# Attention probabilities copied by DMA and transposed as float32r in a hybrid encoder step

## The chip, the cores and the metric

The kernel runs on one core of a Trainium2 chip. A core has a matrix engine (TensorE; PE in the profile, its weight loads PEld), a vector engine (VectorE, DVE), an activation engine (ScalarE, ACT), a general engine (GpSimd, POOL) and a queue engine (SyncE, SP) that here issues nearly all transfers; 16 DMA engines move the data. The metric is the device time of one execution in microseconds (us), the median of several. TensorE works from the on-chip memory SBUF and writes to the accumulators, PSUM; the other engines read PSUM from there.

Two types matter. Both have four bytes. A tile of type float32 ("F32") is multiplied by TensorE at full precision. A tile of type float32r ("F32R") is multiplied with a shortened mantissa. The kernel keeps nearly float32 accuracy in its projections by splitting each operand into a high and a low F32R part and adding three products.

## The reference, cut to what matters

One layer: a pre-normed input of 1024 new rows and 32 rows of running streams is projected to queries, keys, values, forget gates, the conv input and four gates. Attention and a causal convolution module run side by side, are gated, projected, mixed and added to the input. What the change touches is causal attention with 16 heads of width 64:

```python
def fox_attend(q, k, v, cq, ck, qpos, kpos):
    s = jnp.einsum('bqhd,bkhd->bhqk', q.astype(jnp.float32), k.astype(jnp.float32))
    bias = jnp.transpose(cq, (0, 2, 1))[:, :, :, None] - jnp.transpose(ck, (0, 2, 1))[:, :, None, :]
    mask = qpos[:, None] >= kpos[None, :]
    s = jnp.where(mask[None, None], s + bias, jnp.finfo(jnp.float32).min)
    p = jax.nn.softmax(s, axis=-1)
    o = jnp.einsum('bhqk,bkhd->bqhd', p, v.astype(jnp.float32))
    return o.astype(v.dtype)
...
def layernorm(x, g, b):
    xf = x.astype(jnp.float32)
    mu = jnp.mean(xf, axis=-1, keepdims=True)
    xc = xf - mu
    y = xc * lax.rsqrt(jnp.mean(xc * xc, axis=-1, keepdims=True) + EPS) * g.astype(jnp.float32) + b.astype(jnp.float32)
    return y.astype(x.dtype)
```

## The kernel before, in words

The program has three stages. In the first (up to about 605 us) the input is normed and transposed, and the projections for the conv input, the values, the keys, the queries and the attention gates are made; their results go to scratch tensors in HBM (`s_q`, `s_k`, `s_v`, `s_ga`). In the second (about 605 to 1100 us) attention runs, and the projections of the other three gates are mixed into it as filling work for TensorE. In the third the three output projections run.

**The attention loop.** `seq` holds 128 `Block`s, eight per head: block `i` has the 128 queries from row 128·i and the (i+1)·128 keys up to the diagonal. Four `Sample`s for the running streams are put between them. TensorE's order in this stage is the order in which the code is written (`manual_schedule(engines={E.PE})`); the queues of ACT, DVE, POOL and SP are set by a scheduler that runs while the kernel is built. Step `n` of the loop does four things: it starts the scores of block n+3, turns the probabilities of block n, runs four steps of the filler (`fill(4)`: twelve matmuls of a gate projection, line L102, with the single PSUM buffer of the pool `pq`), and, two steps after every fourth block of a head, multiplies by the values.

**One block.** `Block.scores` (L905, L906) puts the scores into one of two PSUM buffers (tag `S`). DVE adds the diagonal mask (L908) and takes the row maximum (L910). ACT takes the exponential into an SBUF tile `P` of type F32 and sums the rows (L913); `P` has three buffers. DVE inverts the sums (L915) and POOL scales `P` in place (L916). `Block.turn` transposes `P` in pieces of 128 by 128 (L926): TensorE loads the piece as its weights and streams the 128 columns of the identity `ident` through it. ACT and DVE copy the result to `pt` (L929). `Block.values` multiplies `pt` by `V` (L940), both F32. All 16 heads together have 16·36 = 576 pieces.

**What is loaded.** `Head.load` brings one head's queries and keys in eight transfers of up to 256 KB (L768 to L775), five steps ahead, and for each second head the values of two heads, `V` (L778, two buffers). The result of two heads goes to `s_o` (L953). The gate results go out by L754, and the weights of the filler come in by L85. All these share SP's queue, which issues in order: a transfer that waits for its data or its buffer holds up those behind it.

**The convolution in the attention stage.** The taps of the last conv input (f = 7) run on DVE during attention, one at a time, as the filler's `beat()` allows. The tile `shift`, subtracted from the conv output before the sums of the layer norm, is read back from `s_m` into a tile of its own at the start of the stage.

Of the kernel before, what the change touches and what calls it, by code (L numbers as in the profile page):

```python
# [48 lines left out]
def build(tc, xT, xt, wv, wf, ckT, cv, clT, stT, vec, cst, yT, kT, vO, lfO, cpT, csT):  # L49
# [195 lines left out]
    def sums(f):  # L245
        return [lambda: from_shift(f, sides["y", f]), lambda: into_sums(f, sides["y", f])]
# [104 lines left out]
    nc.vector.memset(eps_t, EPS)  # L351
    ident = cp.tile([128, 128], F32, name="ident")
    smask = cp.tile([128, TS], F32, name="smask")
# [83 lines left out]

    nc.vector.tensor_copy(ident, cst_t[:, C_ID:C_ID + 128])
    u0 = u_tile(0)
# [318 lines left out]
    class Head:  # L758
# [3 lines left out]
        def load(self):  # L762
# [12 lines left out]
            nc.sync.dma_start(f32(KA[64:68]), s_ak[h])  # L775
            if h % 2 == 0:
                self.V = heads[h + 1].V = hp.tile([128, 8, 128], F32, name="V", tag="V")
                nc.sync.dma_start(self.V, s_v[:, :, 64 * h:64 * h + 128].rearrange("b t d -> t b d"))  # L778

# [27 lines left out]
    cvt[0] = pool("cv7", 1, stack=p2, side="right")  # L807
    taps.extend(last + sums(7))
    psS = pool("psS", 2, stack=p2, space=PS)
# [78 lines left out]
    class Block:  # L888
# [5 lines left out]
        def scores(self):  # L894
# [15 lines left out]
            nc.vector.tensor_reduce(nm[:, 0:1], ps[:, :nb, :w], axis=AX.XY, op=ALU.max, negate=True)  # L910
            self.P = P = ap.tile([128, T], F32, name="P", tag="P", bufs=3)
            with tc.issue_after(sides["tables"].ins):
                nc.scalar.activation(P[:, :nk].rearrange("p (b w) -> p b w", b=nb), ps[:, :nb, :w], AF.Exp,  # L913
                                     bias=nm[:, 0:1], accum_out=nm[:, 1:2])
            nc.vector.reciprocal(nm[:, 2:3], nm[:, 1:2])  # L915
            nc.gpsimd.tensor_scalar(P[:, :nk], P[:, :nk], nm[:, 2:3], 1.0, op0=ALU.mult, op1=ALU.mult)  # L916

        def turn(self):
            i, P = self.i, self.P
            pt_ = PT[i // 4]  # L920
            qo = slice((i % 4) * 128, (i % 4) * 128 + 128)
            for u in range((i + 4) // 4):
                nj = min(4, i + 1 - 4 * u)
                pt = psT.tile([128, 512], F32, name="ptr2", tag="T")
                for j in range(nj):
                    nc.tensor.transpose(pt[:, 128 * j:128 * j + 128],  # L926
                                        P[:, 128 * (4 * u + j):128 * (4 * u + j) + 128], ident)
                put = nc.vector.tensor_copy if u else nc.scalar.copy
                put(pt_[:, 4 * u:4 * u + nj, qo], pt[:, :128 * nj].rearrange("p (j q) -> p j q", j=nj))  # L929

        def values(self):
# [20 lines left out]
            if e == 1 and c == 1:  # L952
                nc.sync.dma_start(s_o[self.head.h // 2, :, :T], ot)  # L953

    PT = [ap.tile([128, 4 * n, 512], F32, name=f"pt{n}", bufs=1) for n in (1, 2)]
# [26 lines left out]
    def layernorm():  # L982

        shift = sides["shift"]
        for _ in range(4):
# [3 lines left out]
        def put(sl, ps):  # L989
            t = t352("t", 3)  # L990
            nc.scalar.activation(t, mean[:, sl], AF.Square)
            nc.vector.scalar_tensor_tensor(rstd[:, sl], ps, 1.0 / D, t, op0=ALU.mult, op1=ALU.subtract)
            nc.vector.tensor_add(mean[:, sl], mean[:, sl], shift[:, sl])
            nc.vector.tensor_scalar(rstd[:, sl], rstd[:, sl], EPS, None, op0=ALU.add)
# [15 lines left out]
    ln = layernorm()  # L1010
    sides["shift"] = ap.tile([128, TT], F32, name="shift", bufs=1)
    nc.sync.dma_start(sides["shift"], s_m)
    start(seq[0])
    fill(8)
    start(seq[1])
    fill(4)
    start(seq[2])
    for n, b in enumerate(seq):
        if n + 3 < len(seq):
            start(seq[n + 3])  # L1020
        if n + 5 < len(seq) and getattr(seq[n + 5], "i", 1) == 0:
            seq[n + 5].head.load()
        if n + 6 < len(seq) and isinstance(seq[n + 6], Sample):
            seq[n + 6].load()
        if isinstance(b, Sample):
# [221 lines left out]
```

## Time and profile before

| what | value |
|---|---|
| time, median of 3 runs | 1402.85 us (1401.42 to 1404.89) |
| the profiled execution | 1405.11 us, its span 1403.3 us |
| granted TensorE clock, mean | 0.999 |
| TensorE busy, whole span | 1390.1 us (99%) |
| TensorE busy from 612 to 1090 us | 476.77 of 478 us |
| DMA share from 612 to 1090 us | 0.46, 129 GB/s |
| transposes of `P` | 576, mean record 273 ns, busy 84.2 us together |

The span is the profiled time from the first to the last instruction; the profiled execution's own time is 1.8 us longer. A record of a matmul begins when its operands are fetched, and its end is modelled, so records of neighbours overlap. What one matmul costs in a stream is therefore read from the distance of starts, not from the length of a record.

### The profile page before, as it was taken

Reading aid. Unit: us, or ns where it says so; the run is one execution under the profiler, and the core shown is the slowest. Engines: PE = TensorE matmul, PEld = TensorE weight load, DVE = VectorE, ACT = ScalarE, POOL = GpSimd, SP = SyncE. Lnnn points to the kernel's source line nnn. Section 1 sums busy time; section 2 is a strip of 40 time slices with the busy share of each in tenths; the row PEclk is TensorE's granted clock in tenths of the full one; section 3 lists DMA queues with packets and bytes.
Section 4 is the critical chain, followed back from the end, with each engine's and each line's share of the span. In section 5 each row is a group of like instructions: output and inputs, shape, how many; then the busy total and the mean of one; then the engine's idle time right before and its main releaser. Section 6 shows DMA issues by size and latency. Waiting matters only on the chain.

```text
span 1403.3 us, 23422 instructions
## 1 busy us (share of the span) xinstructions
PE 1390.1 (99%) x8999; PEld 1303.6 (93%) x8999; DVE 866.0 (62%) x1199; ACT 604.2 (43%) x1180; POOL 617.5 (44%) x541
## 2 busy tenths in 40 slices
PE   8999999999999999999999999999999999999999
PEld 7999999999999999998888888878888999999998
DVE  6687787888898998646655656644444497132111
ACT  6322334646464642245454546544554455232100
POOL 2324254557585875343433433232332366254320
PEclk9999999999999999999999999999999999999999
DMA  4242333424342484335545546353532778444431
GB/s 181 92 141 92 119 108 99 160 76 142 106 152 92 138 194 150 111 100 129 148 107 160 146 136 177 101 154 109 155 115 73 276 254 271 143 138 142 150 108 47
DMA packets 102288, 192.77 MB, mean 137 GB/s; under 512 B 17248, under 2 KB 70368, under 8 KB 102176
## 3 DMA queue, kind: packets, MB, share of 16 engines
q1 hardware_dynamic: 102032, 191.21, 44.4%
q8 instruction: 71, 1.16, 0.4%
q14 instruction: 41, 0.34, 0.1%
q10 hardware_dynamic: 144, 0.07, 0.0%
HBM read 125.58 MB, written 65.64 MB: 136 GB/s over the span
## 4 chain that ended last, share of the span: by engine, by line
PE 92%; issue 3%; DVE 2%; ACT 2%; POOL 1%; DMA 1%; SPq 0%; ACTq 0%; POOLq 0%; DVEq 0%
PE pj L102 67%; PE pjv L582 7%; PE po L940 5%; PE ptr L926 4%; PE psS L905 3%; PE psS L906 2%; POOL wl L94 1%; PE pst L698 1%; PE pst L697 1%; PE po L885 0%; DVE y L1082 0%; PE ptx L427 0%; DMA xtok<-xt 0%; ACT xh L429 0%; PE pjs L541 0%
## 5 line engine op out<-in xcount | busy, mean ns | idle before, releaser
L102 PE MATMUL pj<-xh,wh 128*128 128x352 f32 (+2 forms) x1536 | 510.0, 332 | 1.7 <-ACT t L753 1.1
L102 PE MATMUL pj<-xh,wl 128*128 128x352 f32 (+2 forms) x1536 | 494.0, 322 | 1.9 <-POOL wl L94 1.9
L102 PE MATMUL pj<-xl,wh 128*128 128x352 f32 (+2 forms) x1536 | 495.5, 323 | 0.2
L94 POOL TENSOR_TENSOR wl<-raw,wh 128x384 fp32r<-128x384 f32 (+1 forms) x258 | 323.1, 1280 | 258.1 <-ACT wh L91 226.9
L258 DVE SCALAR_TENSOR_TENSOR y<-u,vec_t,y 128x1086 f32<-128x1086 f32 x240 | 382.5, 1594 | 23.7 <-ACT y L255 19.6
L102 PEld LDWEIGHTS pj<-xh,wh 128*128 128x128 f32 x1536 | 289.0, 188 | 10.2 <-ACT t L753 6.6
L102 PEld LDWEIGHTS pj<-xh,wl 128*128 128x128 f32 x1536 | 289.9, 189 | 2.5 <-POOL wl L94 2.2
L102 PEld LDWEIGHTS pj<-xl,wh 128*128 128x128 f32 x1536 | 289.1, 188 | 1.4 <-DVE xl L430 1.2
L916 POOL TENSOR_SCALAR P<-P,nm 128x128 f32<-128x128 f32 (+7 forms) x128 | 107.6, 842 | 283.3 <-DVE nm L915 216.9
L91 ACT CAST wh<-raw 128x1024 fp32r<-128x1024 f32 x86 | 90.1, 1048 | 111.2 <-PE pj L102 80.5
L913 ACT ACTIVATE P<-psS,nm 128x128 f32<-128x128 f32 (+7 forms) x128 | 95.4, 745 | 70.7 <-DVE nm L910 61.5
L910 DVE TENSOR_REDUCE nm<-psS 128x1 f32<-128x128 f32 (+7 forms) x128 | 96.8, 756 | 8.6
L908 DVE TENSOR_TENSOR psS<-psS,cmask 128x128 f32<-128x128 f32 x128 | 38.1, 297 | 100.3 <-PE psS L906 99.3
L929 ACT COPY pt<-ptr 128x512 f32<-128x512 f32 (+3 forms) x128 | 65.0, 508 | 75.8 <-PE ptr L926 75.1
L715 POOL TENSOR_TENSOR ql<-qn,qh 128x352 fp32r<-128x352 f32 (+1 forms) x48 | 66.0, 1374 | 68.0 <-ACT qh L714 54.9
L926 PE MATMUL ptr<-ident,P 128*128 128x128 f32 x576 | 84.2, 273 | 0.0
L940 PE MATMUL po<-pt,V 128*64 128x512 f32 (+1 forms) x384 | 75.8, 530 | 0.0
L926 PEld LDWEIGHTS ptr<-ident,P 128*128 128x128 f32 x576 | 69.1, 140 | 5.6 <-issue 0.4
L582 PE MATMUL pjv<-vwh,xh 128*128 128x260 f32 x256 | 72.5, 283 | 0.0
L582 PE MATMUL pjv<-vwl,xh 128*128 128x260 f32 x256 | 72.4, 283 | 0.0
L582 PE MATMUL pjv<-vwh,xl 128*128 128x260 f32 x256 | 72.3, 282 | 0.0
L905 PE MATMUL psS<-KB,QB 128*128 128x256 f32 (+2 forms) x192 | 70.1, 366 | 0.6 <-ACT t L751 0.6
(200 smaller groups left out, 2237.4 us busy)
## 6 DMA issues: line engine op xcount, KB each, us to landing
raw<-wf SPq DMA_DIRECT2D x88, 512.0 KB
QB<-s_q SPq DMA_DIRECT2D x32, 256.0 KB
KB<-s_k SPq DMA_DIRECT2D x32, 256.0 KB
kT<-qn SPq DMA_DIRECT2D x8, 528.0 KB
s_ga<-t SPq DMA_DIRECT2D x24, 176.0 KB
s_gb<-t SPq DMA_DIRECT2D x24, 176.0 KB
s_ma<-t SPq DMA_DIRECT2D x24, 176.0 KB
s_mb<-t SPq DMA_DIRECT2D x24, 176.0 KB
```

Source lines behind the costliest of these rows:

```text
L91: nc.scalar.copy(wh, raw)
L94: nc.gpsimd.tensor_sub(wl[:, k0:k1, :], raw[:, k0:k1, :], f32(wh[:, k0:k1, :]))
L102: nc.tensor.matmul(ps, a[:, kt, :], b(kt, sl), start=(first and n == 0), stop=(last and n == N - 1))
L258: t = nc.vector.scalar_tensor_tensor(y, u[:, i:i + CW], w, y, op0=ALU.mult, op1=ALU.add)
L582: nc.tensor.matmul(ps[:, :VC], a, b, start=(n == 0), stop=(n == 23))
L715: nc.gpsimd.tensor_sub(ql[:, :n], qn[:, o], f32(qh[:, :n]))
L905: nc.tensor.matmul(ps[:, b, :wm], QB[:, qsl], KB[:, ksl], start=True, stop=False)
L910: nc.vector.tensor_reduce(nm[:, 0:1], ps[:, :nb, :w], axis=AX.XY, op=ALU.max, negate=True)
L913: nc.scalar.activation(P[:, :nk].rearrange("p (b w) -> p b w", b=nb), ps[:, :nb, :w], AF.Exp, bias=nm[:, 0:1], accum_out=nm[:, 1:2])
L916: nc.gpsimd.tensor_scalar(P[:, :nk], P[:, :nk], nm[:, 2:3], 1.0, op0=ALU.mult, op1=ALU.mult)
L926: nc.tensor.transpose(pt[:, 128 * j:128 * j + 128], P[:, 128 * (4 * u + j):128 * (4 * u + j) + 128], ident)
L940: nc.tensor.matmul(po[64 * o:64 * o + 64, q0:], V[:, j + o, hd], p[:, j + o, q0:], start=(j == 0), stop=(j == njb - 2), skip_group_check=True)
```

## The change

Five things are changed, all of them for the attention stage.

1. A new tile `R` of type F32R, three buffers. After POOL has scaled `P`, a transfer on SP's queue copies `P` to `R`, bit for bit (`f32(self.R[...])` is the same memory seen as F32). `P` has two buffers now.
2. `turn` reads `R`, and the transposes have F32R operands: `R` as weights, `ident_r` as the stream. The identity tile is now F32R, and `ident` is its F32 view for the other transposes.
3. Scores are started four blocks ahead. `Head.load` and `Sample.load` move by one step as well.
4. `V` has one buffer. Its load (`load_v`) is taken out of `Head.load`: the first stays there, the next ones are issued behind the values of the last block of two heads.
5. `shift` has no tile of its own. After the last tap of f = 7, `shift_again` reads it into the slot of that conv input, `u`.

```diff
-    ident = cp.tile([128, 128], F32, name="ident")
+    ident_r = cp.tile([128, 128], F32R, name="ident")
+    ident = f32(ident_r)
...
-            if h % 2 == 0:
-                self.V = heads[h + 1].V = hp.tile([128, 8, 128], F32, name="V", tag="V")
-                nc.sync.dma_start(self.V, s_v[:, :, 64 * h:64 * h + 128].rearrange("b t d -> t b d"))
+            if h == 0:
+                self.load_v()
+
+        def load_v(self):
+            h = self.h
+            self.V = heads[h + 1].V = hp.tile([128, 8, 128], F32, name="V", tag="V", bufs=1)
+            nc.sync.dma_start(self.V, s_v[:, :, 64 * h:64 * h + 128].rearrange("b t d -> t b d"))
...
-    taps.extend(last + sums(7))
+
+    def shift_again():
+        sides["shift"] = u7p.tile([128, UW], F32, name="u", tag="u")
+        nc.sync.dma_start(sides["shift"][:, :TT], s_m)
+        return 0.1
+
+    taps.extend(last + [shift_again] + sums(7))
...
-            self.P = P = ap.tile([128, T], F32, name="P", tag="P", bufs=3)
+            self.P = P = ap.tile([128, T], F32, name="P", tag="P", bufs=2)
...
             nc.gpsimd.tensor_scalar(P[:, :nk], P[:, :nk], nm[:, 2:3], 1.0, op0=ALU.mult, op1=ALU.mult)
+            self.R = ap.tile([128, T], F32R, name="R", tag="R", bufs=3)
+            nc.sync.dma_start(f32(self.R[:, :nk]), P[:, :nk])
 
         def turn(self):
-            i, P = self.i, self.P
+            i, P = self.i, self.R
...
-                    nc.tensor.transpose(pt[:, 128 * j:128 * j + 128],
-                                        P[:, 128 * (4 * u + j):128 * (4 * u + j) + 128], ident)
+                    nc.tensor.transpose(pt[:, 128 * j:128 * j + 128].bitcast(F32R),
+                                        P[:, 128 * (4 * u + j):128 * (4 * u + j) + 128], ident_r)
...
             if e == 1 and c == 1:
                 nc.sync.dma_start(s_o[self.head.h // 2, :, :T], ot)
+                if self.head.h < H - 1:
+                    heads[self.head.h + 1].load_v()
...
     start(seq[2])
+    start(seq[3])
     for n, b in enumerate(seq):
-        if n + 3 < len(seq):
-            start(seq[n + 3])
-        if n + 5 < len(seq) and getattr(seq[n + 5], "i", 1) == 0:
-            seq[n + 5].head.load()
-        if n + 6 < len(seq) and isinstance(seq[n + 6], Sample):
-            seq[n + 6].load()
+        if n + 4 < len(seq):
+            start(seq[n + 4])
+        if n + 6 < len(seq) and getattr(seq[n + 6], "i", 1) == 0:
+            seq[n + 6].head.load()
+        if n + 7 < len(seq) and isinstance(seq[n + 7], Sample):
+            seq[n + 7].load()
```

**TensorE at the start of the attention stage.** Before, the scores of blocks 2 and 3 (384 and 512 columns) and then the turn of block 0:

```order
L905 MATMUL psS<-KB,QB 128x384
L906 MATMUL psS<-KA,QA 128x384
L905 MATMUL psS<-KB,QB 128x512
L906 MATMUL psS<-KA,QA 128x512
L926 MATMUL ptr_6532<-ident,P 128x128
L102 MATMUL pj<-xh,wh 128x352
```

And with the change:

```order
L916 MATMUL psS<-KB,QB 128x384
L917 MATMUL psS<-KA,QA 128x384
L916 MATMUL psS<-KB,QB 128x512
L917 MATMUL psS<-KA,QA 128x512
L916 MATMUL psS<-KB,QB 128x320
L917 MATMUL psS<-KA,QA 128x320
L916 MATMUL psS<-KB,QB 128x320
L917 MATMUL psS<-KA,QA 128x320
L939 MATMUL ptr_6552<-ident,R 128x128
```

The scores of block 4 (two halves of 320 columns) now stand ahead of the first turn, and the turn reads `R`. The filler stands where it stood.

**SP's queue where a new pair of heads begins.** Before, around the load of `V` (`raw` is a filler weight, `s_ma` a gate result, `QB`, `KB`, `QA`, `KA` the next head; numbers tell buffers apart):

```order
L85 DMA raw_9614<-wf 128x1024
L754 DMA s_ma_64<-t_9094 128x352
L778 DMA V_9567<-s_v_59 128x8x128
L953 DMA s_o_70<-ot_8316 128x1024
L950 DMA ga_9683<-s_ga_66 128x1024
L768 DMA QB_9556<-s_q_57 64x1024
L754 DMA s_ma_64<-t_9249 128x352
L769 DMA QB_9556<-s_q_57 64x1024
L770 DMA KB_9558<-s_k_58 64x1024
```

And with the change:

```order
L783 DMA V_10020<-s_v_59 128x8x128
L929 DMA R_9986<-P_9982 128x768
L85 DMA raw_10559<-wf 128x1024
L966 DMA s_o_70<-ot_9106 128x1024
L846 DMA kc_10053<-ckT 128x2x512
L769 DMA QB_10414<-s_q_57 64x1024
L770 DMA QB_10414<-s_q_57 64x1024
L771 DMA KB_10416<-s_k_58 64x1024
L772 DMA KB_10416<-s_k_58 64x1024
L773 DMA QA_10413<-s_q_57 64x1024
L929 DMA R_10039<-P_10035 128x896
```

The copies of `P` stand among the loads: that of the block with 896 keys has five pieces of a head's queries and keys, a cache load and `s_o` right ahead of it.

**ACT's queue in the same stage**, with what each instruction waits for (a name that begins with DMAHW is a transfer). Before:

```order
L945 COPY ot_9009<-po_9676 64x512 [waits PE_49]
L929 COPY pt2_6437<-ptr2_9699 128x4x128 [waits PE_49]
L913 ACTIVATE P_9695,nm_9693<-psS_9689,nm_9693 128x256 [waits DVE_49,PE_49,Pool_49]
L929 COPY pt2_6437<-ptr2_9738 128x4x128 [waits PE_49]
L913 ACTIVATE P_9734,nm_9732<-psS_9728,nm_9732 128x384 [waits DVE_49,PE_49,Pool_49]
L753 COPY t_9762<-pj_9710 128x352 [waits PE_49]
```

And with the change:

```order
L942 COPY pt2_6437<-ptr2_9870 128x4x128 [waits PE_49]
L924 ACTIVATE P_9864,nm_9862<-psS_9858,nm_9862 128x384 [waits DMAHW1_49,DVE_49,Pool_49]
L942 COPY pt2_6437<-ptr2_9909 128x4x128 [waits PE_49]
L924 ACTIVATE P_9903,nm_9901<-psS_9897,nm_9901 128x512 [waits DMAHW3_49,DVE_49,Pool_49]
L754 COPY t_9933<-pj_9881 128x352 [waits PE_49]
```

Each exponential now waits for a transfer, the copy that frees its buffer of `P`, and the filler's copies out of PSUM (L753, now L754) stand behind exponentials in the same queue.

More of the change, by code (lines that the diff above doesn't have):

```diff
@@ L436, in x_split @@
                 behind.pop(0)()
-    nc.vector.tensor_copy(ident, cst_t[:, C_ID:C_ID + 128])
+    nc.vector.tensor_copy(ident_r, cst_t[:, C_ID:C_ID + 128])
     u0 = u_tile(0)
@@ L982, in layernorm @@
     def layernorm():
-        shift = sides["shift"]
         for _ in range(4):
@@ L992, in put @@
             nc.vector.scalar_tensor_tensor(rstd[:, sl], ps, 1.0 / D, t, op0=ALU.mult, op1=ALU.subtract)
-            nc.vector.tensor_add(mean[:, sl], mean[:, sl], shift[:, sl])
+            nc.vector.tensor_add(mean[:, sl], mean[:, sl], sides["shift"][:, sl])
             nc.vector.tensor_scalar(rstd[:, sl], rstd[:, sl], EPS, None, op0=ALU.add)
@@ L1010, in build @@
     ln = layernorm()
-    sides["shift"] = ap.tile([128, TT], F32, name="shift", bufs=1)
-    nc.sync.dma_start(sides["shift"], s_m)
     start(seq[0])
```

## The prediction

> **What bounds the kernel now.** I read the page's head first, then the table of stages, then who waits in the attention stage, then TensorE's timeline.
>
> ```profile
> span 1403.3 us, 23422 instructions
> PE 1390.1 (99%) x8999; PEld 1303.6 (93%) x8999; DVE 866.0 (62%) x1199; ACT 604.2 (43%) x1180; POOL 617.5 (44%) x541
> 612.00:1090.00 478.00, 476.77 (x3119) 405.07 (x3119) 263.31 (x582) 240.95 (x531) 169.30 (x192) 1.00 0.46 129
> 960.00:1000.00 40.00, 39.96 (x254) 34.24 (x253) 18.68 (x46) 20.71 (x46) 13.57 (x18) 1.00 0.68 182
> PE pj L102 <- ACT t L753: 0.8, 1, 0.8
> ```
>
> The third and fourth lines are stretches (start:end, length, busy time of PE, PEld, DVE, ACT and POOL, granted clock, DMA share, GB/s); the last is the only wait of PE between 612 and 1090 us. TensorE hardly waits there, at full clock, and DVE, ACT and POOL are busy for at most 55% of the stage. So the stage lasts as long as TensorE's instructions need, and a nanosecond taken off each of the 576 transposes is 0.576 us off the end, until something else comes late.
>
> **What a transpose costs, and why.** Distances of starts count, not lengths of records.
>
> ```profile
> L926 PE MATMUL ptr<-ident,P 128*128 128x128 f32 x576 | 84.2, 273 | 0.0
> 904.94 1.04 PE L926 MATMUL ptr<-ident,P 128*128 128x128 f32 x8
> 280.89 0.60 PE L636 MATMUL ptr<-ident,lf 128*16 128x128 f32 x4
> 280.74 0.47 PEld L636 LDWEIGHTS ptr<-ident,lf 128*16 128x16 f32 x4
> L926 PEld LDWEIGHTS ptr<-ident,P 128*128 128x128 f32 x576 | 69.1, 140 | 5.6 <-issue 0.4
> 14.70 0.28 PE L102 MATMUL pj<-xh,wh 128*128 128x256 f32 x1
> 14.82 0.28 PE L102 MATMUL pj<-xh,wl 128*128 128x256 f32 x1
> 14.94 0.28 PE L102 MATMUL pj<-xl,wh 128*128 128x256 f32 x1
> 42.75 0.35 PE L102 MATMUL pj<-xl,wh 128*128 128x416 f32 x1
> ...
> 43.31 0.35 PE L102 MATMUL pj<-xl,wh 128*128 128x416 f32 x1
> L102 PE MATMUL pj<-xh,wl 128*128 128x352 f32 x1488 | 478.4, 322 | 1.9 <-POOL wl L94 1.9
> L978 PE MATMUL psn<-mean,ones_f 128*128 128x352 f32 x6 | 2.4, 476 | 0.0
> ```
>
> Eight transposes last 1.04 us from the first start to the last end; less one record of 0.273 that is seven steps, so (1.04 − 0.273)/7 = 0.110 us each. Four transposes of the forget gates (L636) give the same (0.60 − 0.27)/3 = 0.11 us, though their weights have 16 columns and not 128. So the weight load does not set the step; the 128 streamed columns do, at 0.11/128 = 0.86 ns a column.
>
> The F32R matmuls of L102 stream cheaper: 0.12 us for 256 columns, and (43.31 − 42.75)/3 = 0.187 us for 416. The line through both has (0.187 − 0.12)/160 = 0.42 ns a column, half of the above. L978 agrees: a plain F32 matmul of 352 columns leaves two records (six for three matmuls) of 476 ns where F32R leaves one of 322, and the extra 154 ns are again 0.44 ns a column. F32 streams each column twice, F32R once.
>
> **The change part by part.**
>
> *Transposes as F32R.* The line goes on to 0.12 − 128·0.42 ns = 0.066 us at 128 columns. No row has F32R with fewer than 256 columns, so this is bounded from both sides: at best the transpose halves wholly, 0.055 us; at worst short streams lose the F32R rate and cost what a plain F32 matmul does, two records of two passes, 2·0.110 = 0.22 us. I take 0.066, the end of the line that four widths make. 576·(0.110 − 0.066) = 25.3 us off; the bounds give 31.7 us off and 63 us on.
>
> The Trainium skill ("TensorE: Matmul & The Clock Gate", section "Back-to-back issue gap") gives about 81 ns per matmul for a stream of pairs of weight load and 128-column matmul. By that the transposes would save 576·(0.110 − 0.081) = 16.7 us, an estimate from the page; its figure is not for F32R, and the rows above neither show nor exclude it.
>
> *The copies.* 128 copies of 64 to 512 KB, 4 bytes·128 rows·128 columns·576 = 37.7 MB. In the stage 129 GB/s take a DMA share of 0.46, so 37.7 MB over 478 us (79 GB/s) add about 0.28: 0.74 on average and 0.96 in the fullest stretch above. TensorE does not wait for bytes but for the last copy of its block. What covers a copy is the time between POOL's end and the turn:
>
> ```profile
> 922.67 0.39 PE L905 MATMUL psS<-KB,QB 128*128 128x512 f32 x1
> 927.04 1.53 POOL L916 TENSOR_SCALAR P<-P,nm 128x1024 f32<-128x1024 f32 x2 [2.47 <-DVE nm L915]
> 934.47 1.04 PE L926 MATMUL ptr<-ident,P 128*128 128x128 f32 x8
> 935.59 0.48 ACT L913 ACTIVATE P<-psS,nm 128x256 f32<-128x256 f32 x1
> 987.12 1.91 POOL L916 TENSOR_SCALAR P<-P,nm 128x768 f32<-128x768 f32 x2
> 989.59 0.60 PE L926 MATMUL ptr<-ident,P 128*128 128x128 f32 x4
> 0.74 0.86 SPq L325 DMA_DIRECT2D xtok<-xt  x2
> 4.80 1.06 ACT L380 ACTIVATE sq<-xtok 128x1024 f32<-128x1024 f32 x1 [2.35 <-DMA xtok<-xt]
> ACT sma L1125 <- DMA sma<-s_ma: 16.4, 9, 4.7
> 923.56 0.45 SPq L768 DMA_DIRECT2D QB<-s_q  x1
> SPq L754 <- ACT t L753: 174.3, 44, 9.3
> ```
>
> In the usual case (first three lines) POOL is done by 928.6 and the turn starts at 934.47: at least 5.9 us of slack. In the worst that I found, POOL works two blocks off until 989.03 and the turn starts at 989.59: 0.6 to 1.5 us. Scores one block earlier add a mean step of (1090 − 612)/132 = 3.6 us to every slack: 9.5 usual, 4 to 5 worst. A copy costs, by the first load of the program, 4.80 − 0.74 = 4.1 us with another of the same size beside it. The nearest rows bound it: the 0.45 us of its issue alone at one end, and at the other 4.7 us, the longest that ACT waited for a 176 KB piece behind other loads. I take 3 us free and 5 to 8 us behind a head's eight loads, where 1.3 MB stand in the queue. That fits into 9.5 us and not always into 4 to 5. SP itself has room: 128·0.45 = 58 us of issuing against 174 us in which it waits for gate results; but a copy behind such a wait inherits it. I charge 3 us for a few late copies.
>
> *`P` with two buffers.* The exponential of block m+2 now waits for the copy of block m. In the rows above POOL leaves the block with 1024 keys by 928.6, and the exponential two blocks on (256 keys) starts at 935.59: 7 us for a copy of 3 us, hidden. If the copy takes 8 us, the exponential is late by a microsecond, and behind it on ACT stands the filler's copy out of the one buffer of `pq`, for which TensorE waits next. This is in the 3 us.
>
> *Scores four ahead.* Nothing is added to TensorE's work. At the start of the stage the scores of block 4 need the PSUM buffer of block 2:
>
> ```profile
> 612.58 0.40 PE L906 MATMUL psS<-KA,QA 68*128 68x512 f32 x1
> 613.47 0.58 ACT L913 ACTIVATE P<-psS,nm 128x384 f32<-128x384 f32 x1
> ```
>
> Block 3's scores are issued by 612.8, the exponential of block 2 ends at 614.05, and the turn of block 0 now stands behind: 1.2 us lost once. The first copy (POOL done at about 610) has until 615 and is hidden.
>
> *`V` with one buffer, `shift` in another's slot.* `V` is loaded behind the last values of its two heads, some four blocks (4·3.6 = 14 us) before its first use; a 512 KB load took 4.1 us above. `shift` holds DVE once for a load of that size; DVE is busy for 263 of 478 us. I cost both at nothing; without that cover they would be 4 us each, seven times and once.
>
> **The sum**, against the profiled execution's own 1405.1 us: 1405.1 − 25.3 + 3 + 1.2 = 1384.0. The median of the runs lies 2.3 us lower, so 1381.7: I say **1382 us**, 1.5% faster. With other sizes of the same case (0.055 to 0.075 us a transpose, 0 to 8 us of late copies) it lies between 1374 and 1392.
>
> **The rivals.**
>
> *Two passes whatever the type.* The transposes are a mode of their own: their 128-column weight loads take 140 ns, those of all other matmuls 188. If that mode and not the type sets two passes for four-byte data, the step stays 0.110 and the change only adds 3 + 1.2 us and some crowding: 1407 to 1411, say 1409, slower. It decides if the step measures above about 0.103 us, where 576 times the gain no longer pays the 4.2 us. Against it: the same two passes are seen outside the mode (L978), and F32R loses one there. Chance 0.15.
>
> *Late copies.* The copies wait in the loads' bursts, ACT's queue stops behind an exponential, and the filler's buffer is not emptied. Point from which it decides: copies that take over 9 us from POOL's end in most heads. For it: the DMA share of 0.96 in the fullest stretch and the order of SP's queue, which puts the two largest copies of a head behind 1.3 to 2.3 MB of loads. Against it: 40 us windows with 0.68 are the fullest, and usual slack is 9.5. Three blocks in each of 16 heads late by 0.3 us are 14 us: 1382 + 14 − 3 = 1393; by 1 us, 48 us, all that is won and more. Chance 0.15, of which 0.03 ends slower and 0.02 level. The Trainium skill ("DMA: Bandwidth & Descriptors", section "Queues, rings and completion order") says that each DMA engine takes the descriptors of a queue's ring in order; that is how a copy would inherit the loads ahead of it. No row here shows it by itself.
>
> *The weight load as a floor.* Each transpose has a load of its own. In this mode a load takes 140 ns for 128 columns and about 88 ns for 16 (L636: four in 0.47 us), so 128 columns are some 60 ns of it, close to the 54 ns that the F32R stream would need. If the two overlap only in part, the step ends between 0.066 and 0.110; the middle, 0.088, takes 576·0.022 = 12.7 us off: 1405.1 − 12.7 + 4.2 − 2.3 = 1394. Against it: at 256 columns loads of 188 ns run at a step of 0.12 without a sign of it. Chance 0.12.
>
> The page's 81 ns, above, would be such a floor; by it the time would be 1390, an estimate.
>
> *Short F32R streams at the full F32 cost.* 0.22 us a transpose: 576·0.110 = 63 us on: 1405.1 + 63 + 4.2 − 2.3 = 1470. For it: the lowest width with F32R in the rows is 256, the scores of block 0 among them, which have 128 keys and stream 256. Against it: between 256 and 416 columns the cost is a straight line. Chance 0.08.
>
> **How the numbers follow.** The forecast has 0.50. Differences within 0.3% (4.2 us) cannot be told from none here. Faster: 0.50, the floor's 0.12 and 0.10 of the late copies, 0.72. Slower: the short streams' 0.08, 0.10 of the two passes and 0.03 of the late copies, 0.21. No change: the remaining 0.05 of the two passes and 0.02 of the late copies, 0.07. The range goes from 1372 (best step, no late copy) to 1410 (no gain on TensorE, the copies paid): it leaves out the short streams at full cost and the tails of the others, about 0.15.
>
> **What would show it.** Right: records of the transposes 53 ns shorter and eight of them in about 0.7 us instead of 1.04; the attention stage about 20 us shorter; PE's waits in it a few us, for copies (`R`), for exponentials of `P` or for the filler's buffer. Two passes: the step of 0.110 again. Late copies: the step halves, yet the stage is not 20 us shorter, and rows of PE waiting for a DMA of `R` or of ACT waiting for it appear. The forecast is wrong if the step lies outside 0.055 to 0.075 us or PE waits over 10 us in the stage.

## The result, and the profile after

The changed kernel takes 1452.4 us (median of 4 runs, 1450.61 to 1456.42); the kernel before, on the same chip, takes 1402.92 us (1401.42 to 1404.89). The ratio is 1.0356, with a 95% interval of 1.0331 to 1.0381. The forecast was 1382 us with a range of 1372 to 1410: the sign was wrong, and the time lies 42 us above the range.

The first rows answer those that the prediction began with: the head of the page of the changed kernel, its stage (start:end, length, busy time of PE, PEld, DVE, ACT and POOL, granted clock, DMA share, GB/s), and PE's waits in the stage (total us, times, longest).

```profile
span 1448.4 us, 23698 instructions
PE 1394.1 (96%) x8999; PEld 1303.5 (90%) x8999; DVE 866.8 (60%) x1199; ACT 601.3 (42%) x1180; POOL 619.9 (43%) x541
```

```profile
612.00:1140.00 528.00, 484.62 (x3131) 407.06 (x3131) 262.21 (x576) 237.65 (x530) 171.81 (x190) 0.97 0.64 191
```

```profile
PE psS L916 <- ACT P L924: 24.0, 11, 4.4
PE pj L102 <- ACT t L754: 10.0, 11, 2.0
PE ptr L939 <- DMA R<-P: 5.2, 3, 2.2
```

Before, PE was idle for 478 − 476.77 = 1.2 us of the stage. Now it is idle for 528 − 484.62 = 43.4 us, and the granted clock has gone from 1.00 to 0.97. DVE, ACT and POOL do what they did. Little of the idle time is put down to a transfer directly (`R`, 5.2 us). Most of it is put down to ACT: to exponentials (L924), without which the scores have no PSUM buffer, and to the filler's copies (L754). (In this kernel only ACT and DVE read PSUM; no instruction of POOL does.) One has to ask ACT what it waited for, and SP's queue as well:

```profile
ACT P L924 <- DMA R<-P: 90.2, 39, 6.0
SPq L929 <- POOL P L927: 93.5, 67, 5.4
SPq L929 <- PE ptr L939: 55.3, 36, 5.6
```

In 39 of 128 blocks the exponential waits for the copy of the block two before, which has to leave `P` first. The copies themselves wait for POOL, and in 36 cases for the turn that empties a buffer of `R`.

The chain of waits shows one such place (start, length, what). The rows behind it are POOL and SP's queue in the same microseconds, and two windows of the load:

```profile
756.42 8.67 DMA R<-P
...
765.19 0.47 ACT P L924 x2
...
765.95 0.38 POOL P L927
766.35 5.67 DMA R<-P
...
772.12 0.07 ACT P L924
```

```profile
755.12 1.01 POOL L927 TENSOR_SCALAR P<-P,nm 128x896 f32<-128x896 f32 x1 [6.57 <-DVE nm L926]
```

```profile
753.08 0.59 SPq L769 DMA_DIRECT2D QB<-s_q  x1
...
755.77 0.54 SPq L773 DMA_DIRECT2D QA<-s_q  x1
756.42 0.53 SPq L929 DMA_DIRECT2D R<-P  x1
```

```profile
752.00:768.00 16.00, 12.81 (x87) 11.17 (x86) 7.60 (x16) 6.83 (x14) 6.15 (x6) 1.00 1.03 292
768.00:784.00 16.00, 15.13 (x94) 12.25 (x93) 8.22 (x18) 6.95 (x18) 3.46 (x5) 1.00 0.39 138
```

POOL is done with the block of 896 keys at 755.12 + 1.01 = 756.13. Its copy is issued 0.3 us later, behind five loads of the next head, and has landed after 8.67 us. The exponential two blocks on follows at once, POOL scales that block, and its copy of only 64 KB needs 5.67 us behind the rest of the loads. In these 16 us the DMA engines are full (1.03); in the next 16 they run at 0.39. For all copies of the stage, 16 of each size, the time in us from the issue on SP to the last landing, worked out from the trace:

```
KB       64   128   192   256   320   384   448   512
median  4.6   2.0   2.1   2.8   2.5   2.9   7.2   7.9
longest 7.3   3.8   2.1   4.6   4.7   5.4  11.9   9.3
```

In the median the copies of a head's second to sixth block (128 to 384 KB) take 2 to 3 us. Those of its last two blocks and of the first of the next head, which run with the next head's loads, take 4.6 to 7.9. The loads were slowed too: the medians of those of `QB`, `KB` and `QA` went from 4.1, 5.7 and 6.5 us to 5.7, 6.9 and 7.6.

The transposes did become cheaper. The rows are the group and a full turn, of the changed kernel:

```profile
L939 PE MATMUL ptr<-ident,R 128*128 128x128 f32 x576 | 67.1, 246 | 5.6 <-DMA R<-P 5.2 <-ACT pt L942 0.3
908.33 0.81 PE L939 MATMUL ptr<-ident,R 128*128 128x128 f32 x8
```

By the prediction's way of counting the step is (0.81 − 0.246)/7 = 0.081 us, down from 0.110, and not 0.066. (What this mean step hides is shown further below, with the kernels on a transpose's step.)

**Half clock.** Idle time is not all of the loss. The rows are stretches of 3.41 us each, out of the changed kernel:

```profile
798.72:802.14 3.42, 0.77 (x6) 0.62 (x6) 1.89 (x4) 1.15 (x4) 0.48 (x1) 1.00 0.57 211
802.14:805.55 3.41, 3.41 (x17) 3.41 (x16) 1.59 (x3) 0.59 (x1) 0.59 (x1) 0.50 0.28 96
805.55:808.96 3.41, 3.41 (x23) 3.29 (x23) 1.19 (x3) 2.21 (x6) 0.69 (x1) 1.00 0.14 53
692.87:696.28 3.41, 1.82 (x15) 1.85 (x16) 1.14 (x4) 1.63 (x4) 0.37 (x1) 1.00 1.03 301
696.28:699.70 3.42, 3.33 (x24) 2.95 (x24) 3.28 (x7) 1.45 (x5) 0.48 (x1) 1.00 0.60 203
```

Where PE had been idle for 2.65 of 3.41 us, it ran the next 3.41 us at half clock, busy throughout, and was then granted the full clock again. Where it had been idle for 1.6 us, it kept the full clock. The starts of all such windows lie on one grid of 3.413 us. In this run each of the seven stretches in which PE was idle for 2.0 us or more is followed by half clock, and none with 1.8 us or less is. One of these episodes lasts two windows, so that together they are eight windows, 27.3 us, against one before. The Trainium skill ("TensorE: Matmul & The Clock Gate", section "Part 1: The HAM clock gate (the "warmup" mystery)") states free-running windows of 3413 ns, with the throttle after at least one idle window. The trace agrees on length and grid, but not on a whole idle window: 2.0 idle us of 3.41 were enough.

**The account** against the span of before (1403.3 us): idle time of PE 43.4 − 1.2 = +42 us; (27.3 − 3.4)/2 = 12 us of work lost at half clock; cheaper transposes −11 us (next section). That is +43, and the span grew by 45.1; the last 2 us are not accounted for.

### The profile page after: what moved, and what is told of

Read it like the earlier page. It is cut to its first block, busy times and chain, and to the rows that moved or that the text cites. A ratio compares the mean times of both kernels' runs of the same rounds, so it can differ in the third digit from the quotient of the medians.

```text
span 1448.4 us, 23698 instructions
## 1 busy us (share of the span) xinstructions
PE 1394.1 (96%) x8999; PEld 1303.5 (90%) x8999; DVE 866.8 (60%) x1199; ACT 601.3 (42%) x1180; POOL 619.9 (43%) x541
## 4 chain that ended last, share of the span: by engine, by line
PE 77%; DMA 10%; issue 4%; DVE 4%; ACT 3%; POOL 2%; SPq 1%; ACTq 0%; POOLq 0%; DVEq 0%
PE pj L102 58%; DMA R<-P 8%; PE pjv L583 6%; PE po L953 3%; PE psS L916 2%; PE psS L917 2%; PE ptr L939 2%; POOL wl L94 1%; DMA QB<-s_q 1%; ACT P L924 1%; DVE nm L921 1%; PE warm L345 1%; PE pst L699 1%; POOL P L927 1%; PE pst L698 1%
## 5 line engine op out<-in xcount | busy, mean ns | idle before, releaser
L94 POOL TENSOR_TENSOR wl<-raw,wh 128x384 fp32r<-128x384 f32 (+1 forms) x258 | 319.8, 1267 | 275.5 <-ACT wh L91 239.7
L927 POOL TENSOR_SCALAR P<-P,nm 128x128 f32<-128x128 f32 (+7 forms) x128 | 113.2, 885 | 315.5 <-DVE nm L926 294.3
L924 ACT ACTIVATE P<-psS,nm 128x128 f32<-128x128 f32 (+7 forms) x128 | 95.0, 743 | 147.2 <-DMA R<-P 92.9
L926 DVE RECIPROCAL nm<-nm 128x1 f32<-128x1 f32 x128 | 20.4, 160 | 115.2 <-ACT P L924 114.9
L939 PEld LDWEIGHTS ptr<-ident,R 128*128 128x128 f32 x576 | 62.9, 144 | 14.0 <-issue 6.6
L916 PEld LDWEIGHTS psS<-KB,QB 128*128 128x128 f32 x192 | 36.9, 192 | 41.5 <-ACT P L924 30.2
L939 PE MATMUL ptr<-ident,R 128*128 128x128 f32 x576 | 67.1, 246 | 5.6 <-DMA R<-P 5.2
```

The costliest lines, as they stand in the source:

```text
L94: nc.gpsimd.tensor_sub(wl[:, k0:k1, :], raw[:, k0:k1, :], f32(wh[:, k0:k1, :]))
L916: nc.tensor.matmul(ps[:, b, :wm], QB[:, qsl], KB[:, ksl], start=True, stop=False)
L939: nc.tensor.transpose(pt[:, 128 * j:128 * j + 128].bitcast(F32R), P[:, 128 * (4 * u + j):128 * (4 * u + j) + 128], ident_r)
```

## The experiments

Each is timed in three rounds against the kernel before on the same chip (medians of 1402.5 to 1403.4 us).

### The type alone

```diff
-            self.P = P = ap.tile([128, T], F32, name="P", tag="P", bufs=3)
+            self.R = ap.tile([128, T], F32R, name="P", tag="P", bufs=3)
+            P = f32(self.R)
...
-            nc.gpsimd.tensor_scalar(P[:, :nk], P[:, :nk], nm[:, 2:3], 1.0, op0=ALU.mult, op1=ALU.mult)
+            nc.gpsimd.tensor_scalar(self.R[:, :nk], P[:, :nk], nm[:, 2:3], 1.0, op0=ALU.mult, op1=ALU.mult)
```

This is the kernel before; ACT and POOL write the probabilities into an F32R tile, and the transposes are those of the changed kernel. There is no copy.

> The kernel before with nothing changed but the type: ACT and POOL write P as float32r (so the probabilities are rounded to the shorter mantissa, which the change avoids by its copy) and the 576 transposes have float32r operands. No copy, no fourth block ahead, V and shift as before. Theory (late copies): the transposes alone win what the trace of the changed kernel shows where nothing waits, 24 to 25 ns for each piece of a turn but the first, 448 x 25 = 11 us: about 1392 us, ratio 0.992, with no new waits of PE and the clock as before. Rival (float32r transposes are themselves what costs time, through the half-clock windows or the switch to the next matmul): level or slower, 1403 or more.

Measured: 1394.39 us (1392.84 to 1395.73), ratio 0.9938 (0.9923 to 0.9953): faster than both kernels. The rows of TensorE's timeline are the matmul that follows the turn at 934.47 in the kernel before, and a turn with what follows it in this kernel; the last is PE's only wait in this kernel's stage:

```profile
935.26 0.41 PE L102 MATMUL pj<-xh,wh 128*128 128x352 f32 x1
```

```profile
926.27 0.80 PE L928 MATMUL ptr<-ident,P 128*128 128x128 f32 x8
926.91 0.39 PE L102 MATMUL pj<-xh,wh 128*128 128x352 f32 x1
```

```profile
PE pj L102 <- ACT t L754: 3.7, 7, 0.8
```

From the first of eight transposes to the next matmul it takes 0.64 us instead of 0.79. Over all turns (medians by number of pieces, from the last matmul ahead of a turn to the second behind it) the sum falls from 127.8 to 117.0 us, or 10.7 us, and the span from 1403.3 to 1393.1. The saving is about 24 ns for each piece but the first of a turn: 448·24 ns = 10.8 us. So the F32R transposes are worth 8 to 11 us, not 25.3. The price is the one that the expectation names: the probabilities are rounded as they are written. No number here says what that does to the result.

### The copy alone

```diff
-            self.R = ap.tile([128, T], F32R, name="R", tag="R", bufs=3)
+            self.R = ap.tile([128, T], F32, name="R", tag="R", bufs=3)
```

The changed kernel with F32 transposes.

> The changed kernel with float32 back in the transposes: R is float32, the copy and all else stay. Theory (late copies): the stage is held by the copies, so taking the cheaper transposes away costs between nothing and the 11 us they are worth: 1452 to 1463 us, PE still waits some 40 us for exponentials and the half-clock windows stay. Rival (the float32r transposes cause the half-clock windows or the waits): clearly faster than the changed kernel, under 1440.

Measured: 1460.78 us, ratio 1.041 (1.0388 to 1.0432). PE's waits in this kernel are those of the changed one, so the type has nothing to do with them:

```profile
PE psS L916 <- ACT P L924: 26.1, 11, 6.5
PE pj L102 <- ACT t L754: 11.5, 13, 2.9
```

With the copy in place the type is worth 1460.8 − 1452.4 = 8.4 us, as without it.

### All but the copy

```diff
-            nc.gpsimd.tensor_scalar(P[:, :nk], P[:, :nk], nm[:, 2:3], 1.0, op0=ALU.mult, op1=ALU.mult)
             self.R = ap.tile([128, T], F32R, name="R", tag="R", bufs=3)
-            nc.sync.dma_start(f32(self.R[:, :nk]), P[:, :nk])
+            nc.gpsimd.tensor_scalar(self.R[:, :nk], P[:, :nk], nm[:, 2:3], 1.0, op0=ALU.mult, op1=ALU.mult)
```

> The changed kernel without the copy: POOL writes the scaled probabilities straight into R as float32r (rounded to the shorter mantissa). Four blocks ahead, two buffers of P, one of V, shift in the other slot all stay. Theory (late copies): with the copy gone all of the loss is gone and the 11 us of the transposes stay: 1389 to 1395. Rival (scores four ahead, V single or shift in the conv slot cost time): over 1400, with PE waiting for V, kc or shift.

Measured: 1399.14 us, ratio 0.9974 (0.9962 to 0.9986). PE waits in the stage:

```profile
PE pj L102 <- ACT t L754: 4.0, 9, 0.7
PE psS L859 <- DMA kc<-ckT: 1.8, 3, 1.2
PE psS L916 <- ACT P L924: 1.7, 2, 1.3
```

The copy thus costs 1452.4 − 1399.1 = 53 us. The other parts of the change together give up some 5 us of what the type wins; I had expected nothing of the kind, and the time lies outside the 1389 to 1395 of my theory and just short of the rival's 1400.

### Four blocks ahead

```diff
     start(seq[2])
+    start(seq[3])
...
-        if n + 3 < len(seq):
-            start(seq[n + 3])
+        if n + 4 < len(seq):
+            start(seq[n + 4])
```

The kernel with the type alone, with the order of the changed kernel, loads included.

> The kernel before with P written as float32r, no copy, and only the order changed: scores four blocks ahead. If the 4.7 us between the changed kernel without its copy (1399.1) and the kernel before with the type alone (1394.4) come from the order, this gives 1397 to 1400; if they come from V with one buffer, from shift or from R beside P, it gives 1393 to 1396.

Measured: 1399.93 us (1398.35 to 1404.64), ratio 0.9982 (0.9973 to 0.9992). The order alone costs the 5 us. PE's waits in the stage are now these, and the last row is one of ACT's:

```profile
PE psS L906 <- ACT P L915: 3.2, 5, 1.3
PE psS L849 <- DMA kc<-ckT: 3.0, 2, 1.7
PE pj L102 <- ACT t L754: 0.5, 2, 0.4
ACT P L915 <- PE ptr L928: 35.4, 35, 2.0
```

PE's waits add up to 6.7 us against the 3.7 us of three blocks ahead. Scores that are due earlier meet an exponential that is not done in five places, not once at the start. One thing differs from the changed kernel: here the turn frees the three buffers of `P`, and in 35 blocks the exponential waits for it. So it is likely, but not shown, that `V` with one buffer, `shift` and a separate `R` cost nothing in the changed kernel; no row there has PE wait for `V` or `shift`.

### The copies in another queue

```diff
-            nc.sync.dma_start(f32(self.R[:, :nk]), P[:, :nk])
+            nc.gpsimd.dma_start(f32(self.R[:, :nk]), P[:, :nk])
```

> The changed kernel with the copies issued on POOL's queue in place of SP's; the same bytes by the same DMA engines. Theory (late copies: the copies stand behind a head's loads in SP's queue): the copy lands in 2 to 4 us at any time, ACT's waits for R<-P (90 us) fall below 20, PE's waits below 10, time 1393 to 1408. Rival (the bytes themselves are too many for the DMA engines, or a copy is slow anyway): still over 1435.

Measured: 1480.19 us, ratio 1.0539 (1.0514 to 1.0564). My theory, that the copies are late because they stand behind loads in SP's queue, missed by 72 us. The rows are ACT's and PE's waits, the traffic of POOL's own queue (packets, MB, share) and a piece of the chain:

```profile
ACT P L924 <- DMA R<-P: 99.8, 47, 5.3
PE psS L916 <- ACT P L924: 43.4, 19, 6.5
```

```profile
q0 software_dynamic: 9728, 37.76, 7.7%
```

```profile
768.37 7.74 DMA R<-P
```

All 37.76 MB went through a queue of their own, and a copy still takes 7.74 us beside a head's loads. What is shared is behind the queues. The three largest copies of a head land in 4.5, 8.0 and 8.9 us (medians, worked out as above), each later than in SP's queue; why, and whether this is all of the 28 us that this kernel takes more than the changed one, stays open. The Trainium skill ("DMA: Bandwidth & Descriptors", section "Queues, rings and completion order") says that each DMA engine goes round the queues that have work for it, so another queue would get the copies a turn among the loads and not an engine of their own. The 7.74 us agree with that. My prediction had used the other half of that section, the order within a ring, which this run shows not to be what decides.

### Loads spread over four steps, first attempt

```diff
-        if n + 6 < len(seq) and getattr(seq[n + 6], "i", 1) == 0:
-            seq[n + 6].head.load()
+        for m in range(4):
+            k = n + 10 - m
+            if 9 < k < len(seq) and getattr(seq[k], "i", 1) == 0:
+                seq[k].head.load_some(m)
```

`load_some(m)` issues two of a head's eight transfers.

> The changed kernel, with a head's eight loads of queries and keys issued two at a time in four steps, ten to seven blocks ahead, instead of all eight in one step. Shared engines (the copies of the two or three largest blocks land late because 1.3 MB of a head's loads run on the same 16 DMA engines at the same moment): the copies of blocks with 896 and 1024 keys land in 4 to 5 us instead of 8, PE's waits in the attention stage fall from about 45 us below 20, time 1400 to 1425. Rival (the ring is too short whatever the loads do: exponential, scaling, copy and turn with two buffers of P and three of R leave no room for any copy): waits stay above 35 us, time over 1440.

Measured: 1451.23 us, ratio 1.0335 (1.0306 to 1.0363), which is the changed kernel's time. Read as it stands, this would speak for the rival. But the trace shows that the edit did not do what it says. The rows are SP's queue, and its load in the stretch that holds them:

```profile
758.70 1.24 SPq L777 DMA_DIRECT2D QB<-s_q  x2
...
766.66 0.27 SPq L777 DMA_DIRECT2D KA<-s_ak  x1
```

```profile
757.00:773.00 16.00, 12.88 (x88) 11.24 (x87) 8.21 (x17) 7.09 (x15) 6.15 (x6) 1.00 1.03 298
```

The eight transfers still leave within 8.2 us: the place in the code does not set SP's order here, the scheduler does. The run tells nothing about spreading.

### No loads for 14 heads

```diff
-            seq[n + 6].head.load()
+            h = seq[n + 6].head
+            if h.h == 1:
+                h.load()
+            else:
+                h.q = heads[h.h % 2].q
```

> The changed kernel without the loads of queries and keys of heads 2 to 15: these heads reuse the tiles of heads 0 and 1, so the results of 14 heads are those of other queries and keys; the amount of work on the engines is the same. Shared engines: the copies land in 2 to 4 us throughout, PE's waits in the attention stage fall below 10 us, time 1395 to 1408. Rival (the ring is too short by itself): PE's waits above 30 us, time over 1430.

Measured: 1402.15 us, ratio 0.999 (0.9981 to 0.9999). The copies of 448 and 512 KB land in 3.1 us (medians), and the stage looks like this (the waits are those of PE and ACT):

```profile
612.00:1095.00 483.00, 474.40 (x3149) 398.97 (x3148) 264.00 (x578) 240.90 (x531) 171.95 (x191) 1.00 0.47 162
```

```profile
PE pj L102 <- ACT t L754: 6.0, 10, 2.1
PE psS L916 <- ACT P L924: 2.1, 3, 1.4
ACT P L924 <- DMA R<-P: 41.2, 28, 4.2
```

With all 128 copies in place only 3 us are left of the copy's 53 (1402.2 against 1399.1). The ring of two `P` and three `R` is long enough for copies of 3 us, though not with much to spare: ACT still waits 28 times. Copies and head loads do the damage together.

### Loads spread behind the copies

```diff
+        if n + 4 < len(seq) and 1 <= getattr(seq[n + 4], "i", 0) <= 4 and 1 <= seq[n + 4].head.h < H - 1:
+            with tc.issue_after(seq[n + 4].copy.ins):
+                heads[seq[n + 4].head.h + 1].load_some(seq[n + 4].i - 1)
```

`issue_after` fixes an order in SP's queue without a wait: two of the next head's transfers stand behind each copy of blocks 1 to 4.

> The changed kernel, with a head's eight loads of queries and keys queued two at a time behind the copies of blocks 1, 2, 3 and 4 of the head before (the first attempt at spreading them left the transfers in one burst, because the scheduler of the build put them together again). All bytes are still moved. Collision (the largest copies are late because a head's loads run beside them): the copies with 896 and 1024 keys land in 3 to 5 us, PE's waits in the attention stage fall from about 45 us below 20, the clock back to 0.995 or more, time 1400 to 1420. Rival (the sum of bytes, or the many transfers in SP's queue, wherever they stand): the delay moves to the copies of blocks 1 to 4, waits stay above 30 us, time over 1435.

Measured: 1424.68 us (1422.98 to 1428.21), ratio 1.0159 (1.0139 to 1.018), between the two theories. The rows are the same 16 us as in the changed kernel, and the waits of PE and ACT:

```profile
752.00:768.00 16.00, 16.00 (x109) 14.27 (x109) 8.96 (x20) 7.85 (x19) 4.86 (x8) 1.00 0.78 233
```

```profile
PE pj L102 <- ACT t L754: 17.5, 13, 4.0
PE psS L921 <- ACT P L929: 3.1, 3, 1.7
ACT P L929 <- DMA R<-P: 87.6, 46, 5.2
```

The copies of 448 and 512 KB now land in 3.7 and 3.1 us (medians), and 28 of the 53 us come back with the same bytes moved. But the copies of 192 and 256 KB, which now have the loads beside them, went from 2.1 and 2.8 us to 3.8 and 5.0. ACT waits for copies as long as ever, in more and smaller pieces, and PE's wait moved from the scores to the filler, whose copies stand behind those exponentials in ACT's queue. So the burst is about half of the cause. The rest is, as far as these rows show, that a copy beside even two loads takes 4 to 5 us, for which the loop has no room. Bytes and burst cannot be told further apart by these runs. Three buffers for both `P` and `R`, which would lengthen the loop, probably do not fit into SBUF beside the rest; that was not tried.

### What sets a transpose's step

Two kernels on the type alone. In the first each piece is an ordinary F32R matmul with the identity, not a transpose:

```diff
-                    nc.tensor.transpose(pt[:, 128 * j:128 * j + 128].bitcast(F32R),
-                                        P[:, 128 * (4 * u + j):128 * (4 * u + j) + 128], ident_r)
+                    nc.tensor.matmul(pt[:, 128 * j:128 * j + 128], P[:, 128 * (4 * u + j):128 * (4 * u + j) + 128],
+                                     ident_r, start=True, stop=True)
```

> The kernel before with P written as float32r and no copy, and with each 128 by 128 piece multiplied by the identity as an ordinary float32r matmul instead of in the transpose mode. The ordinary weight load has a record of 188 ns where that of the transpose mode has 140. Load as a floor (the load of the next weights sets the step of 0.083 us that the transpose mode shows): the step grows to 0.10 to 0.12 us, time 1402 to 1415. A floor that is the same for every pair of load and matmul: 0.083 us again, 1394. Stream alone (0.066 us, the mode adds something): 0.066 to 0.07 us, time 1384 to 1388. Short float32r streams at full F32 cost: 0.22 us, time about 1470.

Measured: 1403.88 us, ratio 1.0006 (0.9997 to 1.0015). In the second, 384 of the 576 pieces stream 192 columns:

```diff
+                    w = 192 if j + 1 < nj else 128
+                    nc.tensor.matmul(pt[:, 128 * j:128 * j + w], P[:, 128 * (4 * u + j):128 * (4 * u + j) + 128],
+                                     ident_w[:, :w], start=True, stop=True)
```

> The kernel of the ordinary float32r matmuls against the identity, with 192 columns streamed instead of 128 for the 384 pieces that have a successor in the same accumulator (the 64 columns too many are overwritten by that successor; the result is the same). There the step was 0.107 us with 128 columns. Load as a floor (the weight load, a record of 191 ns, sets the step): the step stays 0.10 to 0.11 us, since by the line of the wide matmuls 192 columns need only 0.093 us; time 1402 to 1407. Short float32r streams at the F32 price of 0.86 ns a column below 256 columns: 192 columns take 0.165 us, 384 times 0.058 us more, time about 1426.

Measured: 1404.21 us, ratio 1.0005 (0.9996 to 1.0015). The rows are the groups of weight loads in the transpose mode and as ordinary matmuls, and a full turn with 128 and with 192 columns:

```profile
L928 PEld LDWEIGHTS ptr<-ident,P 128*128 128x128 f32 x576 | 61.1, 141 | 5.7 <-issue 0.4
```

```profile
L928 PEld LDWEIGHTS ptr<-ident,P 128*128 128x128 f32 x576 | 79.6, 191 | 3.0 <-issue 0.4
```

```profile
905.58 1.01 PE L928 MATMUL ptr<-ident,P 128*128 128x128 f32 x8
```

```profile
903.26 1.01 PE L931 MATMUL ptr<-ident,P 128*128 128x192 f32 x8
```

Eight pieces take 1.01 us with 128 columns and with 192, so the stream does not set this step of (1.01 − 0.264)/7 = 0.107 us. With the ordinary load (191 ns) the step is 0.107 us; in the transpose mode (141 ns) it is 0.080.

These steps are means over a turn. Worked out from the traces one by one, they fall into two kinds (median ns from the start of a piece to that of the next, by its place in the turn; last, the distance of the starts of two weight loads from the third on):

```
                            1st   2nd   3rd   loads
F32, before                 112   108   108     108
F32R, transpose mode         62    64    85      85
F32R, ordinary, 128 col.     62   111   112     112
F32R, ordinary, 192 col.     91   112   110     112
```

The first step of a turn is free of the loads' pace and costs what the stream does: 62 ns at 128 columns in either mode, 91 ns at 192, where the prediction's line has 66 and 93. From then on (in the transpose mode from the third piece) the steps have the pace of the loads, 85 ns in the mode and 112 outside it, and there it is the same for 128 and 192 columns. So the load is the floor of a run of pieces. A transpose of F32, at 108 to 112 ns in every place, lies above the mode's floor of 85 and is set by its stream; that weights of 16 columns give the same step, as the prediction shows, agrees.

## Why the prediction was wrong

**The step that failed** is the charge of "3 us for a few late copies", with `P` in two buffers called "hidden". The copy costs 53 us by the pair of kernels with and without it. The mechanism was in the text, as the rival of late copies and as the exponential that "is late by a microsecond" with the filler's copy behind it. What was wrong was its size, at three points.

- The copy time of 3 us holds for copies without loads beside them (medians of 2.0 to 2.9 us). Behind a head's loads I took 5 to 8 us, and 7.2 and 7.9 are the medians of the two largest. But I set these against 9.5 us of slack for the turn and charged the late ones as a few, where three copies of every head were sure to run with the loads.
- The slack that decided was not the turn's. PE waited 5.2 us for `R` at a turn, and 34 us for exponentials and filler copies. The exponential of block m+2 needs the copy of m, which needs POOL and a buffer of `R`, which needs the turn of m−3. I priced each link by itself from rows in which none was late. In a loop a late link makes the next one late: 8.67 us and then 5.67 us in the chain above, where I had found 7 us of room for one copy of 3.
- I used the mean DMA share (0.74 predicted, 0.64 measured with a longer stage) and set the fullest stretch of 0.96 against windows of 40 us. What counted were stretches of 16 us such as the one shown, at 1.03.

**Half clock** was no term of the sum at all; idle PE time costs over a quarter more than itself here, 12 us on 42.

**The transposes' term** of 25.3 us was mis-sized: 10.7 us by the turns, 8 to 10 by time and span. The slope of 0.42 ns a column and the two passes of F32 were read rightly, and the line does go on down to 128 columns: 62 ns where the stream alone counts, against 66. What failed is that the stream alone would set the step. The load as a floor, a rival with a chance of 0.12 and a step of 0.088, was right in kind, with a mean step of 0.080 and a pace of 0.085. The evidence against it (loads of 188 ns at a step of 0.12 for 256 columns "without a sign of it") could not exclude a floor of 0.107 below that. The 81 ns of the Trainium skill ("TensorE: Matmul & The Clock Gate", section "Back-to-back issue gap"), which the prediction left out of its sum, agree with the measured mean of 0.080 to 0.081 us of the transpose mode; ordinary pairs, at 0.107, do not. Nor did the whole of the steps come off the end: in the kernel with the type alone the 448 steps inside the turns fall from 49.3 to 33.8 us together, 15.5 us less, but the matmul behind a turn starts 83 ns after the last piece and not 28, which gives 128·55 ns = 7.0 us back. That leaves 8.5 us, or 10.7 with the matmul behind it counted in.

**Two passes whatever the type** and **short streams at the full F32 cost** fell: the steps are 0.080 in the transpose mode and 0.107 at both 128 and 192 columns outside it, neither 0.110 (0.165 at 192 columns) nor 0.22.

**Scores four ahead** were charged 1.2 us once at the start and cost about 5. PE's waits, now five for exponentials and two for `kc` among them, are 3 us of that; the rest is open. **`V` and `shift`** at nothing agree with the rows, which have no wait of PE for either.

**Two slips:** with 0.055 us a transpose and no late copy the terms of the sum give 1372, as the range has it, and not 1374. And a head's eight loads are 1.6 MB (six of 256 KB and two of 16); 1.3 MB is what the five loads ahead of the copy of 896 keys carry. Neither changes the forecast.

Of the signs to look for, "the step halves, yet the stage is not 20 us shorter, and rows of PE waiting for a DMA of `R` or of ACT waiting for it appear" is what the profile shows, but for the step, which fell by a quarter, and with the stage longer instead. The bound "PE waits over 10 us" was crossed four times over. The point from which late copies would decide, over 9 us from POOL's end in most heads, was set too high: worked out from the trace, 12 of the 128 copies took that long, in 8 of the 16 heads, and they and the shorter ones around them were enough.

## What to carry to other kernels

Where a tile only has to be of another type with the same bytes, and the rounding of that type can be borne, let the engine that writes it last write that type: that kernel takes 1394.4 us here, 0.6% less than before, where the same type by way of a copy costs 3.5% more. A transfer put into a loop of buffers is to be priced at the moment when its neighbours in the DMA engines are busiest, and against the whole loop, not against the slack of its nearest reader. And before a run is read as evidence on an order, the trace must show that the order changed.

## What was not expected of the hardware

- A weight load sets the step of a run of short F32R matmuls: loads start 85 ns apart in the transpose mode and 112 ns apart outside it, the same at 128 and 192 columns, while the stream alone costs 62 ns at 128 columns and 91 at 192.
- A copy inside SBUF takes 2.0 us for 128 KB and 2.9 us for 384 KB without a head's loads beside it. One of 448 KB takes 3.1 us in the kernel without these loads and 7.2 us beside a head's 1.6 MB of them (medians), and from another queue it is no faster (8.0 us).
- Half clock comes in windows of 3.413 us on a fixed grid. In the changed kernel 2.0 us of idle PE in one window brought it on and 1.8 us did not. In the kernel with the loads spread behind the copies, half clock followed a window with only 1.04 us of idle time (842.94 to 846.35 us), so this is no sharp rule; what else enters was not tried.
